# Two of the four weight sums of a seven-product tile, made by an adding transfer in a one-core encoder trunk

## The chip, the cores and the metric

The kernel runs on one core of a Trainium2 chip. The metric is the device time in microseconds (us) of one execution, as the median of several runs. The core has five engines that the text names as the profile does: PE (TensorE, matrix products; PEld is its loading of weights), DVE (VectorE), ACT (ScalarE), POOL (GpSimd) and SP (SyncE, which here only issues transfers). Each engine works through its own list of instructions in order, and waits on semaphores for others. Transfers between HBM and SBUF are issued by an engine's queue and carried out by 16 DMA engines.

## The reference

Two layers over 512 frames of 1024 channels: a pooling mixer and then a gated MLP with a causal convolution, chunked attention and then the same kind of MLP. The change lies in the MLP alone:

```python
def conv_ffn(h, w_gate, w_val, conv_w, conv_b, w_out):
    """out = (silu(causal_dwconv3(h W_gate)) * (h W_val)) W_out"""
    S = h.shape[1]
    a = h @ w_gate
    ap = jnp.pad(a, ((0, 0), (CONV_W - 1, 0), (0, 0)))
    a = ap[:, 0:S] * conv_w[0] + ap[:, 1:S + 1] * conv_w[1] + ap[:, 2:S + 2] * conv_w[2] + conv_b
    return (jax.nn.silu(a) * (h @ w_val)) @ w_out
```

The hidden width is 2816, which the kernel cuts into 22 channel tiles of 128.

## The kernel before

Channels lie on the 128 partitions, frames along the free axis. A float32 product is made as three passes over operands that are split into a high and a low part: `split` (L88) has ACT write the high part (L90) and DVE the low part (L91). So every weight chunk passes through ACT and DVE before PE can use it.

**Tiles of an FFN.** `KIND` says how a channel tile's gate and value are made. Tiles 0 to 4 are plain. Tiles 5 to 21, seventeen in each of the two FFNs, are made by `strassen` (L392): gate and value weights, each cut into the two halves of the inputs, form a 2 x 2 block matrix (a11, a12: gate; a21, a22: value), which meets 2 x 2 blocks of activations in seven products instead of eight. A product is 12 matmuls of 128 x 256, so a tile has 84 of them. Four sums of weights are needed, s1 = a21 + a22, s2 = s1 - a11, s3 = a11 - a21, s4 = a12 - s2; DVE makes them at L397 to L400 into two tiles, `sa` (s1, s2) and `sb` (s4, s3). The operands on the activations' side, t1 to t4, are made once for each FFN by `mixed` (L357), partly on POOL.

**Buffers.** The raw weights (gate, value, and the output projection's chunks `wo_r`) share three buffers (tag "wr"). `sa` and `sb` share two (tag "as"), so `sa` of a tile takes the buffer that `sa` of the tile before leaves when its parts are made. The parts come in pieces named by their place: g1 (the gate weights), g2 (`sa`), g3 (`sb`), g4 (a22); they go in turn into two buffer pairs of one ring and one of another.

**Order.** PE's order is written by hand: after each product of a tile some matmuls of the output projection of an earlier group of tiles are issued (`output`, L437), 128 x 512 each, summed into the residual X by DVE (L449). The other engines' orders are laid out beforehand by a scheduler from the data dependences. SP's queue issues all weight loads. A tile's results are x1 (product b11, copied from PSUM by ACT, L417), a (gate, L419 and L428), x5 (t1, L422), y (L424, L425) and v (value, L431 and L434); `hidden` (L300) then makes the convolution, the activation and the parts that the output projection takes.

Of the kernel before, what the change touches and what calls it, by code (L numbers as in the profile page):

```python
"""Hybrid trunk (pool mixer + FFN, chunked attention + FFN) on one NeuronCore.

Activations are kept feature-major: channels on partitions, the 512 frames along
the free axis, so that every projection takes its weights as the stationary operand,
the depthwise convolution and the pooling windows shift along the free axis, and no
transposes are needed between layers. A float32 product runs as three float32r passes
over operands that are split exactly into two 12-bit parts (hi + lo). Most of the FFN's gate
and value projections take seven products of half size instead of eight (Strassen).
"""
# [10 lines left out]
AF = mybir.ActivationFunctionType  # L20
# [23 lines left out]
# Attention: slots between the softmax of a query tile, its transpose and its use; slots by which the projections'  # L44
# products are done; the places of a pair's transposes among its slots.
# [4 lines left out]
# FFN: how a channel tile's gate and value are made (u: plain, from the inputs without 1/rms; p: plain; s: seven  # L50
# products), and the groups in which the hidden tiles enter the output projection.
# [15 lines left out]
def trunk(ctx: ExitStack, tc: tile.TileContext, xt, xT, cols, band, edge, poolw, gv, wout, wqk, wv, wo, rel, out):  # L67
# [9 lines left out]
    # Two banks of 16 float32r tiles that the stages use in turn.  # L77
# [3 lines left out]
    # ---------------------------------------------------------------- helpers  # L81
# [6 lines left out]
    def split(raw, hi, lo, eng=None):  # L88
        """raw = hi + lo, exactly."""
        nc.scalar.activation(hi, raw, AF.Copy)  # L90
        (eng or nc.vector).tensor_sub(lo, raw, hi.bitcast(F32))  # L91

    def split_scaled(src, scale, hi, lo):
        """The parts of src * scale (a column), from a tile in SBUF or PSUM."""
        nc.scalar.activation(hi, src, AF.Copy, scale=scale)
        nc.vector.scalar_tensor_tensor(lo, src, scale, hi.bitcast(F32), op0=OP.mult, op1=OP.subtract)

    def load_split(src, n, name, pool=None, eng=None, tag=(None, None)):
        """A weight chunk [P, n] and its two float32r parts."""
        raw = wp.tile([P, 1024], F32, name=f"{name}_r", tag="wr")  # L100
        if pool:
            hi, lo = (pool.tile([P, n], F32R, name=f"{name}_{c}", tag=t, bufs=2 if t == "as" else 1) for c, t in zip("hl", tag))
        else:
            hi, lo = (wp.tile([P, 1024], F32R, name=f"{name}_{c}", tag=f"w{c}", bufs=2) for c in "hl")
        nc.sync.dma_start(raw[:, :n] if len(src.shape) == 2 else raw.rearrange("p (a b) -> p a b", a=src.shape[1]), src)
        split(raw[:, :n], hi[:, :n], lo[:, :n], eng)
        return hi, lo

    def mm3(o, sh, sl, mh, ml, first, last):
        """o += (sh + sl).T @ (mh + ml), a matmul at a time"""  # L110
        yield nc.tensor.matmul(o, sh, mh, start=first, stop=False)  # L111
        yield nc.tensor.matmul(o, sh, ml, start=False, stop=False)  # L112
        yield nc.tensor.matmul(o, sl, mh, start=False, stop=last)  # L113
# [7 lines left out]
    def rsqrt(a, y, t):  # L121
        """y = a ** -0.5 on a small tile: a seed from exp(-log(a) / 2) and a Newton step."""
# [15 lines left out]
    def frame_rstd(acc, name):  # L138
        """1/rms of each frame, as columns [P, TT]."""
# [8 lines left out]
    def on_all(y, name):  # L148
        """The columns of y, [P, TT], as a row [P, S] on every partition."""
# [10 lines left out]
    # ---------------------------------------------------------------- pool mixer  # L160
    # The window means are products of the frame-major normed input with banded matrices.
    with tc.tile_pool(name="start", bufs=1) as sp:
# [14 lines left out]
        # The tensor engine's clock rises with use: these keep it busy until the input is there.  # L177
# [40 lines left out]
        # Frames [0, 256) come from frame tiles 0, 1; frames [256, 512) from 1, 2, 3.  # L218
# [25 lines left out]
        # Relative-position bias by distance, negated: row h holds, at u, distance u - 127, clipped.  # L244
# [10 lines left out]
    def prepare(XS, c, name):  # L255
        """The parts of x * g (1/rms is applied to the products), and 1/rms."""
        acc = g_tile(f"{name}_acc")
        for k in range(KD):
            split_scaled(X[k], col[:, c + k:c + k + 1], XS[k], XS[KD + k])
        for k in range(KD):  # L260
            sumsq(k, acc, name)
        return acc

    # ---------------------------------------------------------------- gated conv FFN
    # The gate and value projections multiply 2 x 2 blocks of weights (gate or value, halves of the inputs) by 2 x 2
    # blocks of activations (those halves, halves of the frames) in seven products (Strassen, in Winograd's form).
    def ffn(l, first, pool):
# [18 lines left out]
        def parts(raw, n, name, out_=False):  # L286
            """The parts of n columns of weights."""
# [12 lines left out]
        def hidden(f, a, finish):  # L300
            """The parts of silu(conv(a)) * val of a channel tile."""
# [12 lines left out]
        def early():  # L314
            """The first channel tiles, from the inputs without 1/rms."""
# [31 lines left out]
        def blocks(R):  # L347
            """The inputs times 1/rms, and their parts."""
            # They lie in tiles that the weights take later.
# [7 lines left out]
        def mixed(h, i):  # L357
            """The operands that mix blocks."""
# [3 lines left out]
            nc.gpsimd.tensor_sub(t1, b12, b11)  # L362
            nc.vector.tensor_sub(t2, b22, t1)
            nc.vector.tensor_sub(t3, b22, b12)
            nc.gpsimd.tensor_sub(t4, b21, t2)
# [3 lines left out]
        def whole(raw, i, j, names):  # L369
            """The parts of two moving operands, of the channel tiles i and i + 4."""  # L370
# [5 lines left out]
        def plain(f):  # L376
            """The gate and value of a channel tile; yields four times in each."""
# [14 lines left out]
        def strassen(f):  # L392
            """The gate and value of a channel tile; yields after each product."""
            g, v = (raw_tile(f"gv{l}_{f}_{i}", gv[l, f, i]) for i in range(2))
            sa, sb = (sum_tile(f"s{x}{f}") for x in "ab")
            a11, a12, a21, a22, s1, s2, s4, s3 = (x[:, z * S:(z + 1) * S] for x in (g, v, sa, sb) for z in range(2))
            nc.vector.tensor_add(s1, a21, a22)  # L397
            nc.vector.tensor_sub(s2, s1, a11)
            nc.vector.tensor_sub(s3, a11, a21)
            nc.vector.tensor_sub(s4, a12, s2)  # L400
# [20 lines left out]
            w = parts(sa, 1024, f"g2_{f}")  # L421
            nc.scalar.activation(x5, product(w, 0, "t1"), AF.Copy)  # L422
# [4 lines left out]
            w = parts(sb, 1024, f"g3_{f}")  # L427
            nc.vector.tensor_add(a[:, HALF:], y5, product(w, 0, "b22"))  # L428
            yield mm
            o = product(w, 1, "t3")[:, None, :].to_broadcast([P, 2, HALF])  # L430
            nc.vector.tensor_add(val.rearrange("p (h s) -> p h s", h=2), y.rearrange("p (h s) -> p h s", h=2), o)  # L431
# [6 lines left out]
        def output(g):  # L438
            """Adds a group's part of the output projection to the residual, a matmul at a time."""
# [41 lines left out]
    # ---------------------------------------------------------------- chunked attention  # L481
    def attention():
# [3 lines left out]
        # Softmax weights, transposed: [keys, (query tile of the half), key tile, query]; the key tile past  # L486
        # the first query tile's reach stays zero.
# [8 lines left out]
        def products(ov, w, name, eng=None):  # L496
            """ov[t] = the frames of tile t times the columns of w (two channel tiles to a chunk)."""
# [9 lines left out]
        def project(c, banks="PQ"):  # L507
            """Queries and keys of two head pairs, frame-major, with their norms (less the gains)."""
# [21 lines left out]
        def values(half, banks):  # L530
            ov = [psum(banks[t // 2], f"v{half}_{t}", BANKS[banks]) for t in range(TT)]
            yield from products(ov, wv[half], f"wv{half}")
            for t in range(TT):
                for hh in range(2):
                    V[t, 2 * half + hh] = vt = set1[(t * 2 + half) * 2 + hh].rearrange("p (h a d) -> p h a d", h=4, a=2)
                    v4 = ov[t][:, hh * 256:(hh + 1) * 256].rearrange("p (h d) -> p h d", d=HD)
                    # Even heads as [hi | lo], odd heads as [lo | hi].
# [3 lines left out]
        def output(ps_):  # L541
            """Adds the output projection of some of the head pairs to the residual."""
# [16 lines left out]
        def channel_major(p, i):  # L559
            """A pair's queries or keys, channel-major: by head, the queries' hi and lo parts and the keys' hi part twice,  # L560
            on the two halves of the partitions; the keys' lo parts."""
# [11 lines left out]
        def scores(h, t):  # L573
            """Softmax of the query tile t of a head."""
# [10 lines left out]
            # The scores and their bias come negated: their least is the softmax's maximum.  # L585
# [14 lines left out]
        def turn(h, t):  # L600
            """The softmax of a query tile, transposed, in parts."""
# [8 lines left out]
        def mix(h, m):  # L610
            """The values of half a head's frames, mixed."""
# [23 lines left out]
        # One query tile of a head to a slot; its stages lie slots apart, and the products of the next  # L635
        # projections stand between them.
# [4 lines left out]
        with tc.manual_schedule(engines={mybir.EngineType.PE}):  # L641
            cur, done, kept = 0, 0, 0

            def fill(upto):
                """Products of the projections, as many as are due by this point (in slots)."""
# [13 lines left out]
            for i in range(nb + LAG + LAGM):  # L659
# [14 lines left out]
                # The last projection leaves the parts of the input to those of the heads' outputs.  # L674
# [7 lines left out]
    # ---------------------------------------------------------------- program  # L682
# [60 lines left out]
```

## Time and profile before

| | |
|---|---|
| runs | 1034.02, 1032.58, 1029.66 us; median 1032.58 us |
| span of the profiled execution | 1030.7 us; no time of its own is given beside the span |
| DMA traffic | 105.31 MB, mean 102 GB/s |
| DVE sums of weights, L397 to L400 | 4 x 34 instructions of 128 x 512, about 684 ns each |

The span reaches from the first to the last instruction. Busy times of the engines overlap, so they don't add up to it; what an engine's work is worth depends on whether the engine that sets the end waits for it. "Idle before" in a row is the time in which its engine stood still just ahead of it, with the engine and line that ended the wait. A row of the timeline is start, duration, engine, line, operation, out<-in, shape. Instructions on an engine overlap a little, so the distance between two starts, not the duration, is what one costs a busy engine.

### The profile page before, as it was taken

Reading aid. Unit: us, or ns where it says so; the run is one execution under the profiler, and the core shown is the slowest. Engines: PE = TensorE matmul, PEld = TensorE weight load, DVE = VectorE, ACT = ScalarE, POOL = GpSimd, SP = SyncE. Lnnn points to the kernel's source line nnn. Section 1 sums busy time; section 2 is a strip of 40 time slices with the busy share of each in tenths; the row PEclk is TensorE's granted clock in tenths of the full one; section 3 lists DMA queues with packets and bytes.
Section 4 is the critical chain, followed back from the end, with each engine's and each line's share of the span. In section 5 each row is a group of like instructions: output and inputs, shape, how many; then the busy total and the mean of one; then the engine's idle time right before and its main releaser. Section 6 shows DMA issues by size and latency. Waiting matters only on the chain.

```text
span 1030.7 us, 15641 instructions
## 1 busy us (share of the span) xinstructions
PE 1011.2 (98%) x5928; PEld 871.2 (85%) x5928; DVE 815.3 (79%) x1407; ACT 536.3 (52%) x926; POOL 143.5 (14%) x140
## 2 busy tenths in 40 slices
PE   8899999999999999999899999999999999999998
PEld 7678999999999988887676767778899999999986
DVE  6889899988899754443767787889989998989843
ACT  5646554544445443345577867657554454444521
POOL 5413000000000013103324232052100000000000
PEclk8999999999999999999999999999999999999999
DMA  7213343333323234243233333222233333333323
GB/s 251 85 55 112 100 117 99 108 93 113 103 86 107 74 98 143 83 125 106 79 108 103 100 97 103 66 99 82 82 105 109 110 106 98 110 93 91 105 73 110
DMA packets 37724, 105.31 MB, mean 102 GB/s; under 512 B 4464, under 2 KB 6912, under 8 KB 37648
## 3 DMA queue, kind: packets, MB, share of 16 engines
q1 hardware_dynamic: 35984, 99.63, 32.3%
q0 software_dynamic: 1312, 4.24, 1.5%
q8 instruction: 47, 0.77, 0.3%
q10 hardware_dynamic: 352, 0.44, 0.1%
q14 instruction: 29, 0.24, 0.1%
HBM read 95.86 MB, written 2.14 MB: 95 GB/s over the span
## 4 chain that ended last, share of the span: by engine, by line
PE 89%; DVE 4%; issue 1%; ACT 1%; DMA 0%; DVEq 0%; ACTq 0%
PE out L111 8%; PE out L113 8%; PE out L112 8%; PE st_t L111 6%; PE st_t L112 6%; PE st_t L113 6%; PE st_b L111 5%; PE st_b L112 5%; PE st_b L113 5%; PE qk L111 3%; PE gv L112 3%; PE gv L113 3%; PE gv L111 3%; PE qk L113 3%; PE qk L112 3%; PE sc L588 2%
## 5 line engine op out<-in xcount | busy, mean ns | idle before, releaser
L90 ACT ACTIVATE g_h<-gv_r 128x1024 fp32r<-128x1024 f32 x68 | 57.6, 847 | 83.0 <-PE st_t L112 44.6
L113 PE MATMUL out<-one,ow_l 128*128 128x512 f32 x224 | 88.4, 394 | 0.0
L111 PE MATMUL out<-one,ow_h 128*128 128x512 f32 x224 | 88.3, 394 | 0.0
L112 PE MATMUL out<-one,ow_h 128*128 128x512 f32 x224 | 88.2, 394 | 0.0
L90 ACT ACTIVATE ow_h<-wo_r 128x640 fp32r<-128x640 f32 (+1 forms) x64 | 50.5, 788 | 65.4 <-PE out L112 48.5
L449 DVE TENSOR_TENSOR X<-out,X 128x512 f32<-128x512 f32 (+1 forms) x65 | 44.1, 680 | 42.0 <-PE out L113 41.8
L112 PE MATMUL st_t<-h,g_h 128*128 128x256 f32 x272 | 76.7, 282 | 0.0
L112 PE MATMUL st_t<-two,g_h 128*128 128x256 f32 x272 | 76.6, 282 | 0.0
L111 PE MATMUL st_t<-h,g_h 128*128 128x256 f32 x272 | 76.5, 281 | 0.0
L113 PE MATMUL st_t<-two,g_l 128*128 128x256 f32 x272 | 76.5, 281 | 0.0
L111 PE MATMUL st_t<-two,g_h 128*128 128x256 f32 x272 | 76.5, 281 | 0.0
L113 PE MATMUL st_t<-h,g_l 128*128 128x256 f32 x272 | 76.4, 281 | 0.0
L91 DVE TENSOR_TENSOR g_l<-gv_r,g_h 128x1024 fp32r<-128x1024 f32 x68 | 64.9, 954 | 4.9 <-ACT g_h L90 4.0
L90 ACT ACTIVATE g_h<-sa 128x1024 fp32r<-128x1024 f32 x34 | 36.1, 1060 | 59.0 <-PE st_t L112 45.3
L91 DVE TENSOR_TENSOR ow_l<-wo_r,ow_h 128x640 fp32r<-128x640 f32 (+1 forms) x64 | 56.6, 885 | 1.5 <-ACT ow_h L90 1.3
L112 PE MATMUL st_b<-h,g_h 128*128 128x256 f32 x204 | 57.5, 282 | 0.0
L112 PE MATMUL st_b<-two,g_h 128*128 128x256 f32 x204 | 57.4, 282 | 0.0
L111 PE MATMUL st_b<-two,g_h 128*128 128x256 f32 x204 | 57.4, 281 | 0.0
L111 PE MATMUL st_b<-h,g_h 128*128 128x256 f32 x204 | 57.4, 281 | 0.0
L113 PE MATMUL st_b<-two,g_l 128*128 128x256 f32 x204 | 57.4, 281 | 0.0
L113 PE MATMUL st_b<-h,g_l 128*128 128x256 f32 x204 | 57.2, 280 | 0.0
L306 DVE SCALAR_TENSOR_TENSOR c<-a,col,c 128x511 f32<-128x511 f32 x76 | 56.6, 745 | 0.1
(299 smaller groups left out, 3185.4 us busy)
## 6 DMA issues: line engine op xcount, KB each, us to landing
gv_r<-gv SPq DMA_DIRECT2D x88, 512.0 KB, 3.6
wo_r<-wout SPq DMA_DIRECT2D x32, 384.0 KB, 3.2
wo_r<-wout SPq DMA_DIRECT2D x32, 320.0 KB, 2.9
wqk_r<-wqk SPq DMA_DIRECT2D x16, 512.0 KB, 3.6
wv_r<-wv SPq DMA_DIRECT2D x8, 512.0 KB, 3.5
B<-rdram POOLq DMA_DIRECT2D x16, 256.0 KB, 3.6
wo_r<-wo SPq DMA_DIRECT2D x8, 512.0 KB, 3.7
z<-zh SPq DMA_DIRECT2D x24, 128.0 KB, 3.1
```

The source lines that it names most:

```text
L90: nc.scalar.activation(hi, raw, AF.Copy)
L91: (eng or nc.vector).tensor_sub(lo, raw, hi.bitcast(F32))
L111: yield nc.tensor.matmul(o, sh, mh, start=first, stop=False)
L112: yield nc.tensor.matmul(o, sh, ml, start=False, stop=False)
L113: yield nc.tensor.matmul(o, sl, mh, start=False, stop=last)
L306: nc.vector.scalar_tensor_tensor(c[:, j:], a[:, :S - j], cw[2 - j], c[:, j:], op0=OP.mult, op1=OP.add)
L449: nc.vector.tensor_add(X[d][:, fs], o[:, fs], X[d][:, fs])
L588: nc.tensor.matmul(sc[:, :nw], q[hs, t * P:n], kl[hs, :nw], start=False, stop=True)
```

## The change

`sa` now holds s3 and s1 and is filled by two transfers. The first, on SP's queue, writes a21 into both halves. The second, on POOL's queue, reads a11 and a22 from HBM and adds them to what lies there: s3 = a21 + a11, s1 = a21 + a22. It can be issued only when the first has landed. `sb` holds s4 and s2, still made by DVE: s2 = a11 + s1, s4 = a12 + s2. To make every weight sum an addition, the operands t1 to t4 change their signs, and so does the sign with which t3 enters the value. The product t3 now belongs to g2 and comes right after t1; before, it belonged to g3. The gate and value weights are loaded in full as before.

```diff
         def strassen(f):
             g, v = (raw_tile(f"gv{l}_{f}_{i}", gv[l, f, i]) for i in range(2))
             sa, sb = (sum_tile(f"s{x}{f}") for x in "ab")
-            a11, a12, a21, a22, s1, s2, s4, s3 = (x[:, z * S:(z + 1) * S] for x in (g, v, sa, sb) for z in range(2))
-            nc.vector.tensor_add(s1, a21, a22)
-            nc.vector.tensor_sub(s2, s1, a11)
-            nc.vector.tensor_sub(s3, a11, a21)
-            nc.vector.tensor_sub(s4, a12, s2)
+            a11, a12, a21, a22, s3, s1, s4, s2 = (x[:, z * S:(z + 1) * S] for x in (g, v, sa, sb) for z in range(2))
+            w0, w1 = gv[l, f, 0], gv[l, f, 1]
+            row, gap = w1.ap[0], w1.offset - w0.offset
+            sa3 = sa.rearrange("p (a b) -> p a b", a=2)
+            nc.sync.dma_start(sa3, bass.AP(tensor=w1.tensor, offset=w1.offset, ap=[row, [0, 2], [1, S]]))
+            nc.gpsimd.dma_start(sa3, bass.AP(tensor=w0.tensor, offset=w0.offset, ap=[row, [gap + S, 2], [1, S]]), accum_op=OP.add)
+            nc.vector.tensor_add(s2, a11, s1)
+            nc.vector.tensor_add(s4, a12, s2)
...
-            w = parts(sa, 1024, f"g2_{f}")
-            nc.scalar.activation(x5, product(w, 0, "t1"), AF.Copy)
+            ws = parts(sa, 1024, f"g2_{f}")
+            nc.scalar.activation(x5, product(ws, 1, "t1"), AF.Copy)
+            yield mm
+            w = parts(sb, 1024, f"g3_{f}")
+            o3 = product(ws, 0, "t3")[:, None, :].to_broadcast([P, 2, HALF])
             yield mm
             nc.vector.tensor_add(y6, x1, product(w, 1, "t2"))
             nc.vector.tensor_add(y5, y6, x5)
             yield mm
-            w = parts(sb, 1024, f"g3_{f}")
+            nc.vector.tensor_sub(val.rearrange("p (h s) -> p h s", h=2), o3, y.rearrange("p (h s) -> p h s", h=2))
             nc.vector.tensor_add(a[:, HALF:], y5, product(w, 0, "b22"))
-            yield mm
-            o = product(w, 1, "t3")[:, None, :].to_broadcast([P, 2, HALF])
-            nc.vector.tensor_add(val.rearrange("p (h s) -> p h s", h=2), y.rearrange("p (h s) -> p h s", h=2), o)
             w = parts(a22, 512, f"g4_{f}")
...
         def mixed(h, i):
...
-            nc.gpsimd.tensor_sub(t1, b12, b11)
-            nc.vector.tensor_sub(t2, b22, t1)
-            nc.vector.tensor_sub(t3, b22, b12)
-            nc.gpsimd.tensor_sub(t4, b21, t2)
+            nc.gpsimd.tensor_sub(t1, b11, b12)
+            nc.vector.scalar_tensor_tensor(t2, t1, -1.0, b22, op0=OP.mult, op1=OP.subtract)
+            nc.vector.tensor_sub(t3, b12, b22)
+            nc.gpsimd.tensor_add(t4, b21, t2)
```

In the changed program the transfers are L401 and L402, s2 is L403 and s4 L404; y is L431 and L432, v L434 and L438, a L423 and L435, X L453.

In DVE's list of before, between the low parts of g3 of tile 13 and those of g1 of tile 14 in the first FFN, the four sums of tile 14 stand spread among other work (u, c and X belong to `hidden` and `output`):

```order
L91 TENSOR_TENSOR g3_13_l_2415<-sb13_2318,g3_13_h_2414 128x1024
L306 SCALAR_TENSOR_TENSOR c12_2301<-a12_2145,col_124,c12_2301 128x510
L397 TENSOR_TENSOR sa14_2487<-gv0_14_1_r_2485 128x512
L399 TENSOR_TENSOR sb14_2488<-gv0_14_0_r_2483,gv0_14_1_r_2485 128x512
L398 TENSOR_TENSOR sa14_2487<-sa14_2487,gv0_14_0_r_2483 128x512
L435 TENSOR_TENSOR c12_2301<-v12_2148,c12_2301 128x512
L419 TENSOR_TENSOR a13_2323<-x13_2324,st0_13_b21_2348 128x256
L91 TENSOR_TENSOR g4_13_l_2451<-gv0_13_1_r_2315,g4_13_h_2450 128x512
L400 TENSOR_TENSOR sb14_2488<-gv0_14_0_r_2483,sa14_2487 128x512
L91 TENSOR_TENSOR u1l_509<-c12_2301,u1h_508 128x512
L449 TENSOR_TENSOR X2_74<-out0_1_2_2283,X2_74 128x512
```

In the changed DVE list the two sums that are left stand together, and from s2 to the low parts of g2 (made from `sa`) there are ten rows:

```order
L403 TENSOR_TENSOR sb14_2488<-gv0_14_0_r_2483,sa14_2487 128x512
L404 TENSOR_TENSOR sb14_2488<-gv0_14_0_r_2483,sb14_2488 128x512
L453 TENSOR_TENSOR X2_74<-out0_1_2_2283,X2_74 128x512
L91 TENSOR_TENSOR ow0_1_4_l_2537<-wo0_1_4_r_2534,ow0_1_4_h_2536 128x768
L91 TENSOR_TENSOR g1_14_l_2498<-gv0_14_0_r_2483,g1_14_h_2497 128x1024
L431 TENSOR_TENSOR y13_2325<-x13_2324,st0_13_t2_2416 128x256
L432 TENSOR_TENSOR y13_2325<-y13_2325,x13_2324 128x256
L434 TENSOR_TENSOR v13_2326<-st0_13_t3_2392,y13_2325 128x512
L435 TENSOR_TENSOR a13_2323<-y13_2325,st0_13_b22_2436 128x256
L91 TENSOR_TENSOR g2_14_l_2545<-sa14_2487,g2_14_h_2544 128x1024
```

The first sum moved from just behind c of tile 12 to behind the parts of `hidden` of tile 12 (u1l stands right ahead of it now), and it is the first DVE row that needs the transfers.

On SP's queue the new transfer of a tile stands between its weight loads, here for tiles 13 and 14 in the changed program:

```order
L277 DMA gv0_13_0_r_2313<-gv 128x1024
L401 DMA sa13_2317<-gv 128x2x512
L277 DMA gv0_13_1_r_2315<-gv 128x1024
L277 DMA wo0_1_3_r_2406<-wout 128x768
L277 DMA gv0_14_0_r_2483<-gv 128x1024
L277 DMA gv0_14_1_r_2485<-gv 128x1024
L401 DMA sa14_2487<-gv 128x2x512
L277 DMA wo0_1_4_r_2534<-wout 128x768
```

Of before, the same rows stood there without the two of L401; the queue waits at L401 until DVE has made the low parts of `sa` of the tile before, and the value load (tile 13) or the wout load (tile 14) stands behind it.

On POOL, the list of before goes from the operands t1 to t4 straight to the next stage; in the changed program the adding transfers follow, and the first one stands ahead of the last operands:

```order
L362 TENSOR_TENSOR t12_2_857<-hb_624 128x256
L365 TENSOR_TENSOR t34_2_858<-hh1_627,t12_2_857 128x256
L402 DMA sa5_971<-gv 128x2x512
L362 TENSOR_TENSOR t12_3_912<-hb_624 128x256
L365 TENSOR_TENSOR t34_3_913<-hl1_628,t12_3_912 128x256
L402 DMA sa6_1130<-gv 128x2x512
```

Behind these rows POOL's list holds nothing but the adding transfers of tiles 7 to 21 until the FFN ends.

## Prediction

> **What bounds the kernel now.** I read the page's busy times and chain first, then the waits of TensorE (PE), then the stretches by time.
>
> ```profile
> span 1030.7 us, 15641 instructions
> PE 1011.2 (98%) x5928; PEld 871.2 (85%) x5928; DVE 815.3 (79%) x1407; ACT 536.3 (52%) x926; POOL 143.5 (14%) x140
> PE 89%; DVE 4%; issue 1%; ACT 1%; DMA 0%; DVEq 0%; ACTq 0%
> ```
>
> PE is busy for 98% of the span and holds 89% of the chain that ended last. The waits of PE by releaser begin so, and all its rows together make about 15 us:
>
> ```profile
> PE tp L606 <- DVE mx L591: 4.9, 3, 2.4
> PE gv L112 <- DVE one L96: 4.1, 4, 2.3
> ```
>
> Neither is in a seven-product tile: L606 is attention, and the gv products of L112 that wait stand at the start of an FFN. Cut to 100 to 350 us, where the first FFN's seventeen such tiles run, the same view has no row at all. So VectorE (DVE) work that goes there has no PE wait to shorten. Could PE itself run quicker beside a less busy DVE? The stretches answer that (columns: PE, PEld, DVE, ACT, POOL busy with instruction counts, clock, DMA share, GB/s):
>
> ```profile
> 290.00:345.00 55.00, 55.00 (x394) 51.75 (x394) 50.88 (x78) 28.77 (x39) 0.00 (x0) 1.00 0.34 101
> 985.00:1025.00 40.00, 40.00 (x178) 32.48 (x177) 17.86 (x26) 8.77 (x12) 0.00 (x0) 1.00 0.32 98
> L111 PE MATMUL out<-one,ow_h 128*128 128x512 f32 x45 | 17.8, 395 | 0.0
> L113 PE MATMUL out<-one,ow_l 128*128 128x512 f32 x224 | 88.4, 394 | 0.0
> ```
>
> DVE is 93% busy in the first stretch and 45% in the second. The third row is an output matmul in the second stretch (395 ns), the fourth the like over the whole span (394 ns): a free DVE does not speed PE. The gain that this change can bring is therefore about nothing; the question is what the new transfers cost.
>
> **The change, part by part.** Removed are two DVE sums a tile:
>
> ```profile
> L397 DVE TENSOR_TENSOR sa<-gv_r 128x512 f32<-128x512 f32 x34 | 24.5, 721 | 12.0 <-DMA gv_r<-gv 11.8
> L399 DVE TENSOR_TENSOR sb<-gv_r,gv_r 128x512 f32<-128x512 f32 x34 | 23.2, 684 | 0.0
> ```
>
> That is 47.7 us of DVE time, all beside a PE that does not wait: worth 0 on the path. The matmuls stay 84 a tile; t3 before t2, the turned signs, and eight t2 operands as a scalar_tensor_tensor (128x256, some tenths of a us in all) lie beside PE work: 0.
>
> Added is a **loop from tile to tile**. sa of tile f+1 takes the buffer of sa of tile f, which is free when DVE has made the low parts of sa (g2 lo). Before, a plain sum filled it. Now, in turn: SP issues the first transfer; it lands; POOL issues the adding transfer; it lands; DVE runs s2 and, in order behind it, everything up to its next g2 lo. Only then can SP go on. While DVE waits at s2 (L403), g1 lo and the y, v, a sums are queued behind it, and PE waits for g1; ACT waits at the high parts of sa, with c, g3 and x copies behind; SP holds the val or wout load behind its sa transfer. Only the turns of this loop can cost time, when one is longer than PE's tile.
>
> PE's tile: x1 is copied once a tile. First and last of 17 copies in the first FFN:
>
> ```profile
> 104.91 0.39 ACT L417 ACTIVATE x<-st_b 128x256 f32<-128x256 f32 x1 [0.58 <-PE st_b L113]
> 342.06 0.39 ACT L417 ACTIVATE x<-st_b 128x256 f32<-128x256 f32 x1 [0.87 <-PE st_b L113]
> ```
>
> 237.15 us over 16 steps: **14.8 us a tile**.
>
> The DVE part of the loop, s2 to g2 lo, is priced by the distances between starts in a back-to-back piece of before:
>
> ```profile
> 261.04 0.69 DVE L91 TENSOR_TENSOR u3l<-c,u3h 128x512 fp32r<-128x512 f32 x1
> 261.64 0.41 DVE L424 TENSOR_TENSOR y<-x,st_t 128x256 f32<-128x256 f32 x1
> 261.97 0.68 DVE L449 TENSOR_TENSOR X<-out,X 128x512 f32<-128x512 f32 x1
> 262.57 1.22 DVE L91 TENSOR_TENSOR g_l<-gv_r,g_h 128x1024 fp32r<-128x1024 f32 x1
> 263.71 0.42 DVE L425 TENSOR_TENSOR y<-y,x 128x256 f32<-128x256 f32 x1
> 264.04 0.95 DVE L91 TENSOR_TENSOR ow_l<-wo_r,ow_h 128x768 fp32r<-128x768 f32 x1
> 264.91 0.41 DVE L428 TENSOR_TENSOR a<-y,st_b 128x256 f32<-128x256 f32 x1
> ```
>
> A 512 takes 0.60, a 256 0.33, a 768 0.87, a 1024 1.14. Tile 14's ten rows (above, under the change) make 4 x 0.60 + 3 x 0.33 + 0.87 + 1.14 + 1.22 for the last = 6.6 us. The same sum over the 16 loops of an FFN runs from 5.7 to 7.2; mean 6.2.
>
> The transfers:
>
> ```profile
> gv_r<-gv SPq DMA_DIRECT2D x88, 512.0 KB, 3.6
> wo_r<-wout SPq DMA_DIRECT2D x32, 320.0 KB, 2.9
> B<-rdram POOLq DMA_DIRECT2D x16, 256.0 KB, 3.6
> wo_r<-wo SPq DMA_DIRECT2D x8, 512.0 KB, 3.7
> L581 POOL DMA_DIRECT2D B<-rdram x16: 536/559/631, 399.8 to 637.6; - x16
> DMA to landing us min/median/max: 3.3/3.6/6.4
> ```
>
> A hand-over, read where SP takes up a freed buffer:
>
> ```profile
> 277.67 1.22 DVE L91 TENSOR_TENSOR g_l<-gv_r,g_h 128x1024 fp32r<-128x1024 f32 x1
> 278.92 1.74 SPq L277 DMA_DIRECT2D gv_r<-gv  x2
> ```
>
> DVE ends at 278.89 and SP issues 0.03 us later; I take 0.1 for each of four. The first transfer has the size and the 2 KB pieces of wo_r<-wo: 3.7 us. A turn is 3.7 + 0.4 + 6.2 + A = **10.3 + A**, and it hurts from A = 14.8 - 10.3 = **4.5 us** on.
>
> A, the adding transfer from issue to landing, is shown nowhere. The gv and wout rows give 0.7 us for 192 KB, so 1.9 us for 512 KB and 0.9 for 256. POOL's own transfer of 256 KB thus has 3.6 - 0.9 = 2.7 us besides data; a plain one of 512 KB would take 2.7 + 1.9 = 4.6. It also has twice the pieces (256 rows for 128), whose issue takes POOL 0.56 us for 128: up to 0.5 more. And an add must read the old SBUF contents, another 512 KB: between 0 (beside the first read) and 1.9 (after it). So A lies between 4.6 and 7.0; nearest is the middle, half of the second read: 2.7 + 1.9 + 0.5 + 0.9 = **6.0**. Outside bounds: below, 3.6, the half-size row itself; above, 8, its longest landing (6.4) plus 0.9 for the missing 256 KB and 0.7 for half a wout load in flight.
>
> The Trainium skill, "Collectives: The Full Stack", section "The bandwidth ceiling: the fold count and why AG ≠ RS ≠ AR", says that an adding transfer needs two source reads on the same ring and so runs at half the rate, 31 GB/s over two engines. That speaks against this change; an estimate from that page, 512 KB over 16 engines at that rate, is 2.1 us of data, A = 5.3 and some 20 us in all. No trace of before can show it.
>
> PE starts with a lead, read at the first tile:
>
> ```profile
> 102.56 1.22 DVE L91 TENSOR_TENSOR g_l<-sa,g_h 128x1024 fp32r<-128x1024 f32 x1
> 107.76 0.39 ACT L422 ACTIVATE x<-st_t 128x256 f32<-128x256 f32 x1 [0.34 <-PE st_t L113]
> ```
>
> g2 lo ends at 103.8. t1's twelve matmuls end just before 107.76 and, at 0.12 us each, began near 106.1: 2.3 us, and DVE has two sums (1.2 us) less there: 3.5, less 0.5 since g1 is a little tighter than g2: **3 us** for each FFN.
>
> Sum: 2 x (16 x (6.0 - 4.5) - 3) = 2 x 21 = **42 us**. 1030.7 + 42 = 1072.7 for the profiled execution; the median of the runs (1032.6) lies 1.9 above its span, so 1074.6, say **1075**.
>
> POOL's queue at the first tile: the adding transfer stands ahead of the last t1 operand.
>
> ```profile
> 86.10 0.41 DVE L364 TENSOR_TENSOR t<-hl,ha 128x256 f32<-128x256 f32 x1
> 91.64 1.12 POOL L362 TENSOR_TENSOR t<-hb 128x256 f32<-128x256 f32 x1 [2.96 <-DVE two L91]
> ```
>
> sa's buffer is free after L364, 86.5; plus 3.7 is 90.2, before 91.64: 0. Without that cover it would be a us or two, once in each FFN.
>
> **The rivals.**
>
> *Hidden (not slower).* If A is under 4.9, the turns fit: at 4.9 the sum is 2 x (6.4 - 3) = 7 us, about the 0.5% (5 us) that a measurement of this kernel can tell; at 4.5 it is 0, so 1032. For it: the plain estimate is 4.6, and the second read may run beside the first. Against: the pieces double, and the wout load is in flight then. The Trainium skill's "DMA: Bandwidth & Descriptors", section "Anatomy of one DMA — SWDGE (gpsimd) path", gives 2.0 us plus bytes at 436 GB/s, an estimate of 3.2 us here and no cost; by that rule the 256 KB row would be 2.6, and the trace has 3.6.
>
> *POOL starved.* POOL's work can be stretched beside DVE:
>
> ```profile
> 87.94 0.74 POOL L365 TENSOR_TENSOR t<-hh,t 128x256 f32<-128x256 f32 x1 [2.85 <-DVE t L363]
> 96.59 2.93 POOL L365 TENSOR_TENSOR t<-hl,t 128x256 f32<-128x256 f32 x1 [3.83 <-DVE t L363]
> ```
>
> The same instruction takes four times as long. If issuing were stretched so (1.1 to 4.4 us), A would be 9.3 and the sum 2 x (77 - 3) = 148: 1180. Against: POOL's issue in attention stayed within 536 to 631 ns.
>
> *Faster.* If the 47.7 us of DVE time let PE close gaps that the profile files elsewhere, at most about 5 us, 1027. PE's empty wait list for these tiles speaks against it.
>
> **How the numbers follow.** Forecast (A from 4.9 to 8): 0.62. Hidden: 0.27. Starved: 0.08. Faster: 0.03. At A = 8 the sum is 2 x (56 - 3) = 106: 1138. The range takes in hidden and forecast, 1031 to 1138; the forecast's own is 1040 to 1138. Faster by over 0.5%: 0.03; within: 0.27; slower: 0.70.
>
> **What would show it.** Right: x1 copies 16.3 us apart in place of 14.8; DVE's s2 (L403) idle before it, released by a DMA; PE rows at st_b waiting for g1's parts; sa from POOL landing in about 6 us. Wrong: no PE wait in these tiles (A under 4.5); or period and A long, but DVE not waiting at L403, which would put the loop elsewhere, such as in SP's queue.

## The result and the profile after

The changed kernel takes **1138.3 us** (median of 4 runs, 1135.98 to 1142.52) against 1031.9 (4 runs of the kernel before beside it): a ratio of 1.105, 95% interval 1.101 to 1.109. The forecast was 1075, slower; the direction and the mechanism came true, the size did not, and the time lies 0.3 us above the range's upper end of 1138. The span of the profiled execution is 1140.7, 110.0 more than before.

The page of the profile after, cut to what answers the rows of before:

```profile
span 1140.7 us, 15771 instructions
PE 1048.0 (92%) x5928; PEld 899.2 (79%) x5928; DVE 776.6 (68%) x1339; ACT 528.1 (46%) x926; POOL 181.7 (16%) x174
...
q0 software_dynamic: 10560, 22.06, 11.1%
...
PE 42%; DVE 24%; DMA 20%; issue 6%; ACT 2%; DVEq 0%; POOLq 0%; ACTq 0%
...
L403 DVE TENSOR_TENSOR sb<-gv_r,sa 128x512 f32<-128x512 f32 x34 | 23.5, 692 | 189.5 <-DMA sa<-gv 179.1
L113 PE MATMUL st_b<-two,g_l 128*128 128x256 f32 x204 | 66.2, 324 | 73.2 <-DVE g_l L91 73.2
...
sa<-gv SPq DMA_DIRECT2D x34, 512.0 KB, 3.8
sa<-gv POOLq DMA_DIRECT2D x34, 512.0 KB, 7.3
wo_r<-wout SPq DMA_DIRECT2D x32, 384.0 KB, 4.0
```

PE's 89% of the chain has become 42%, and DVE and DMA hold 44%. The row of L403 is the reason: s2 stands idle for 179.1 us until the transfers have filled sa. PE then waits 73.2 us for the low parts of g1, which stand behind s2 in DVE's queue; before, PE had no wait in these tiles. The other 37 us of the 110 show in PE's row as busy time (1048.0 against 1011.2), at a mean granted clock of 0.964 against 0.993; more on it at the end. DVE did lose its two sums (776.6 us busy against 815.3) and nobody gained by it.

One turn of the loop, from the timelines of SP, POOL and DVE in the profile after (the rows between are left out):

```profile
269.37 0.38 SPq L401 DMA_DIRECT2D sa<-gv  x1
...
273.48 1.20 POOL L402 DMA_DIRECT2D sa<-gv  x1 [17.38 <-DMA sa<-gv]
...
281.19 0.69 DVE L403 TENSOR_TENSOR sb<-gv_r,sa 128x512 f32<-128x512 f32 x1 [5.45 <-DMA sa<-gv]
...
286.10 1.22 DVE L91 TENSOR_TENSOR g_l<-sa,g_h 128x1024 fp32r<-128x1024 f32 x1
...
287.35 0.38 SPq L401 DMA_DIRECT2D sa<-gv  x1
```

First transfer to POOL's issue 4.1 us, adding transfer to s2 7.7, s2 to the end of g2 lo 6.1, and SP issues the next 0.03 later: 18.0 us. The x1 copies of the first FFN show the same step:

```profile
104.75 0.39 ACT L421 ACTIVATE x<-st_b 128x256 f32<-128x256 f32 x1
...
396.85 0.36 ACT L421 ACTIVATE x<-st_b 128x256 f32<-128x256 f32 x1
```

292.1 us over 16 steps are 18.3 us a tile; it was 14.8, and 16.3 was forecast. The mean of all 32 turns, from the same rows of every tile, is 18.5. In none of the 32 does DVE stand idle for 0.1 us or more between s2 and the end of g2 lo, and SP's issue follows 0.02 to 0.03 us behind. So the turn closes through transfers, POOL and DVE alone: PE does not lengthen it, however slow its matmuls are.

### The profile page after: what moved, and what is told of

Same layout as the page of the kernel before. It is cut to its first block, busy times and chain, and to the rows that moved or that the text cites. A ratio compares the mean times of both kernels' runs of the same rounds, so it can differ in the third digit from the quotient of the medians.

```text
span 1140.7 us, 15771 instructions
## 1 busy us (share of the span) xinstructions
PE 1048.0 (92%) x5928; PEld 899.2 (79%) x5928; DVE 776.6 (68%) x1339; ACT 528.1 (46%) x926; POOL 181.7 (16%) x174
## 3 DMA queue, kind: packets, MB, share of 16 engines
q0 software_dynamic: 10560, 22.06, 11.1%
## 4 chain that ended last, share of the span: by engine, by line
PE 42%; DVE 24%; DMA 20%; issue 6%; ACT 2%; DVEq 0%; POOLq 0%; ACTq 0%
DMA sa<-gv 18%; DVE g_l L91 7%; PE out L112 3%; PE out L113 3%; PE out L111 3%; PE qk L111 3%; DVE c L306 3%; PE qk L113 2%; PE qk L112 2%; DVE ow_l L91 2%; PE gv L112 2%; DVE sb L403 2%; PE gv L111 2%; PE gv L113 2%; PE sc L592 2%
## 5 line engine op out<-in xcount | busy, mean ns | idle before, releaser
L403 DVE TENSOR_TENSOR sb<-gv_r,sa 128x512 f32<-128x512 f32 x34 | 23.5, 692 | 189.5 <-DMA sa<-gv 179.1
L113 PE MATMUL st_b<-two,g_l 128*128 128x256 f32 x204 | 66.2, 324 | 73.2 <-DVE g_l L91 73.2
L402 POOL DMA_DIRECT2D sa<-gv x34 | 40.9, 1204 | 541.7 <-DVE a L423 142.3
L113 PEld LDWEIGHTS st_b<-two,g_l 128*128 128x128 f32 x204 | 43.4, 213 | 79.2 <-DVE g_l L91 79.1
L304 ACT ACTIVATE c<-a,col 128x512 f32<-128x512 f32 x38 | 31.0, 816 | 139.8 <-DVE a L435 133.5
L113 PE MATMUL out<-one,ow_l 128*128 128x512 f32 x224 | 91.1, 407 | 0.0
L112 PE MATMUL out<-one,ow_h 128*128 128x512 f32 x224 | 90.9, 406 | 0.0
L111 PE MATMUL out<-one,ow_h 128*128 128x512 f32 x224 | 90.4, 403 | 0.0
L453 DVE TENSOR_TENSOR X<-out,X 128x512 f32<-128x512 f32 (+1 forms) x65 | 44.0, 678 | 38.8 <-PE out L113 38.8
L112 PE MATMUL st_b<-h,g_h 128*128 128x256 f32 x204 | 62.2, 305 | 0.0
L111 PE MATMUL st_b<-h,g_h 128*128 128x256 f32 x204 | 62.2, 305 | 0.0
L113 PE MATMUL st_b<-h,g_l 128*128 128x256 f32 x204 | 62.0, 304 | 0.0
L111 PE MATMUL st_b<-two,g_h 128*128 128x256 f32 x204 | 61.3, 300 | 0.0
```

The lines of the kernel that those rows point to most:

```text
L304: nc.scalar.activation(c, a, AF.Identity, scale=cw[2], bias=cw[3])
L402: nc.gpsimd.dma_start(sa3, bass.AP(tensor=w0.tensor, offset=w0.offset, ap=[row, [gap + S, 2], [1, S]]), accum_op=OP.add)
L403: nc.vector.tensor_add(s2, a11, s1)
L453: nc.vector.tensor_add(X[d][:, fs], o[:, fs], X[d][:, fs])
```

## The experiments

The theory is that the serial loop (sa free, first transfer, adding transfer, s2 to g2 lo) sets the tile and so the time. The rivals: the new order and signs; the added load on the DMA engines or a slower PE; and, for the size, what makes the adding transfer take 7.3 us and not 6.0. Intervals are 95% intervals of the ratio to the kernel before, run beside them. The times of the kernel before in these comparisons were 1032.4 (the first four experiments below), 1032.0 (the one with no load in the tiles) and 1031.5 (the other four).

### The order and signs alone

```diff
-            nc.sync.dma_start(sa3, bass.AP(tensor=w1.tensor, offset=w1.offset, ap=[row, [0, 2], [1, S]]))
-            nc.gpsimd.dma_start(sa3, bass.AP(tensor=w0.tensor, offset=w0.offset, ap=[row, [gap + S, 2], [1, S]]), accum_op=OP.add)
+            nc.vector.tensor_add(s1, a21, a22)
             nc.vector.tensor_add(s2, a11, s1)
+            nc.vector.tensor_add(s3, a11, a21)
             nc.vector.tensor_add(s4, a12, s2)
```

> Signs, operands and product order of the change, but all four sums by VectorE again, no added transfers. Loop theory (the serial loop sa free, first transfer, adding transfer, VectorE's stretch to g2 lo sets the tile): no loop, a tile of 14.8 us as before, 1032 (1028 to 1037). Rival 'order' (the new product order or signs cost part of the 106 us): above 1037, up to 1138 if they are all of it.

1032.4 us, ratio 0.9998 (0.998 to 1.002). Order and signs cost nothing; all of the 106 us comes from the transfers.

### s2 and s4 behind g2 lo

Here low[0] is the instruction that made the last low parts.

```diff
-            nc.vector.tensor_add(s2, a11, s1)
-            nc.vector.tensor_add(s4, a12, s2)
...
             ws = parts(sa, 1024, f"g2_{f}")
+            with tc.issue_after(low[0].ins):
+                nc.vector.tensor_add(s2, a11, s1)
+                nc.vector.tensor_add(s4, a12, s2)
```

> All transfers of the change with the same buffers, but s2 and s4 stand behind g2 lo in VectorE's queue, so that VectorE's stretch in the loop shrinks from 6.6 us to about 2.5 (high parts 1.2, low parts 1.2). Loop theory: turn 4.6 + 7.3 + 2.5 = 14.4 against PE's 14.8, so 1032 to 1050, depending on queueing on ScalarE. Rival 'load' (35 MB more traffic or POOL's issuing slows PE's loads or its clock): 1138 as in the change. Rival 'transfer term only' (the stretch on VectorE doesn't count): 1138 too.

1059.8 us, ratio 1.027 (1.023 to 1.031): three quarters of the loss is gone with every transfer and buffer in place, only by the order of DVE's queue. So neither the load nor the transfers by themselves make the 106 us. The time is 10 us above the expected band. The timelines of one turn show two things that were overlooked. DVE's, at g2 lo:

```profile
272.82 1.22 DVE L91 TENSOR_TENSOR g_l<-sa,g_h 128x1024 fp32r<-128x1024 f32 x1
273.96 0.69 DVE L426 TENSOR_TENSOR sb<-gv_r,sa 128x512 f32<-128x512 f32 x1
```

SP's, from there on:

```profile
274.71 0.38 SPq L402 DMA_DIRECT2D sa<-gv  x1
276.27 0.33 SPq L278 DMA_DIRECT2D gv_r<-gv  x1
280.22 0.33 SPq L278 DMA_DIRECT2D wo_r<-wout  x1
```

And ScalarE's, at the high parts of sa:

```profile
286.29 0.84 ACT L90 ACTIVATE ow_h<-wo_r 128x768 fp32r<-128x768 f32 x1 [5.15 <-DMA wo_r<-wout]
287.04 1.05 ACT L90 ACTIVATE g_h<-sa 128x1024 fp32r<-128x1024 f32 x1
```

s2 reads sa as well, and now comes last, so sa is free 0.7 us later than g2 lo (273.96 + 0.69 = 274.65, and SP goes on at 274.71). And ScalarE takes the wout parts ahead of the high parts of sa: the wout load, issued at 280.22, was there at 286.29, after 6.1 us, nearly all of them beside the adding transfer (issued at 278.99, landed 7.1 us later). The turns have a mean of 16.1 us.

### A third buffer for the sums

`into` is a sum buffer of its own, allotted ahead of ha and hb.

```diff
-            return pool.tile([P, 1024], F32R, name=name, tag="as", bufs=2).bitcast(F32)
+            return pool.tile([P, 1024], F32R, name=name, tag="as", bufs=3).bitcast(F32)
...
-        R = big.tile([P, S], F32, name=f"{name}_R")
+        R = into[:, :S]
```

> All transfers of the change and its order, but three buffers in place of two for the sums (1/rms on all partitions moves into one of them, before its use as a sum), so that sa of the next tile waits for a sum of the tile before last. Loop theory: one turn now spans two tiles, 4.6 + 7.3 + about 9 = 21 us against 29.6, so hidden: 1028 to 1037, granted clock back near 0.99. Rival 'load': 1100 to 1138, clock 0.96.

1033.6 us, ratio 1.002 (0.9996 to 1.004), granted clock 0.993. Who waits for POOL's transfer in this kernel, and its landing time (shortest, median, longest), from the view of line 402:

```profile
who waited for it (us, times):
  DVE sb L403: 1.8, 2
DMA to landing us min/median/max: 5.7/6.1/9.6
```

And PE's row, from its waits:

```profile
PE st_b L113 <- DVE g_l L91: 1.3, 3, 0.8
```

The same 68 transfers and the same bytes are all there, and the adding ones take 5.7 to 9.6 us each, but almost nobody waits: 1.8 us in place of 179.1. It is the reuse of sa's buffer that turns the transfers into time, not their load. And with them hidden, DVE's saved sums gain nothing either, as step one of the prediction had it.

### The same transfers without the add

```diff
-            nc.gpsimd.dma_start(sa3, bass.AP(tensor=w0.tensor, offset=w0.offset, ap=[row, [gap + S, 2], [1, S]]), accum_op=OP.add)
+            nc.gpsimd.dma_start(sa3, bass.AP(tensor=w0.tensor, offset=w0.offset, ap=[row, [gap + S, 2], [1, S]]))
```

> POOL's transfer overwrites in place of adding (the sums s1 and s3 are left out), bytes, pieces, queues and waits unchanged. Issue to landing, A, was 7.3 us with the add. My reading (issuing 1.2 of 256 pieces, data 1.9, fixed 2.7) gives A = 5.5 to 6 without it, a turn of 16.7 to 17.2 and 2 x (16 x 1.9 to 2.4 - 3) = 55 to 71: 1087 to 1103. If the add costs nothing: A stays 7.3 and the time 1138. If the add is nearly all of what exceeds the 3.6 us of the 256 KB row: A = 4.6, turn 15.8, 1059.

1062.4 us, ratio 1.030 (1.025 to 1.035), below the value expected and near the 1059 of its last case: the add costs more than I took. From its page:

```profile
q0 software_dynamic: 6208, 22.06, 6.8%
...
L402 POOL DMA_DIRECT2D sa<-gv x34 | 24.6, 725 | 487.8 <-DVE c L439 157.3
...
sa<-gv POOLq DMA_DIRECT2D x34, 512.0 KB, 4.7
```

And the view of line 402:

```profile
DMA to landing us min/median/max: 3.9/4.7/6.7
```

Against the change (10560 packets of q0, 1.20 us of issuing, 7.3 us), this one has 4352 packets less, 128 for each of 34 transfers. So it wasn't only the add that went: without the 1312 packets that q0 has before the change, a plain transfer has 144 and an adding one 272, and POOL issues the plain one in 0.73 us. Its shortest landing is 3.9 us, that of the adding one 5.8: together the add and its packets cost 1.9 us between the two shortest, 0.5 of it in issuing. The mean turn is 16.2 us.

### Half the size

```diff
-            nc.sync.dma_start(sa3, bass.AP(tensor=w1.tensor, offset=w1.offset, ap=[row, [0, 2], [1, S]]))
-            nc.gpsimd.dma_start(sa3, bass.AP(tensor=w0.tensor, offset=w0.offset, ap=[row, [gap + S, 2], [1, S]]), accum_op=OP.add)
+            nc.sync.dma_start(s1, bass.AP(tensor=w1.tensor, offset=w1.offset, ap=[row, [1, S]]))
+            nc.gpsimd.dma_start(s1, bass.AP(tensor=w1.tensor, offset=w1.offset + S, ap=[row, [1, S]]), accum_op=OP.add)
             nc.vector.tensor_add(s2, a11, s1)
             nc.vector.tensor_add(s4, a12, s2)
+            nc.vector.tensor_add(s3, a11, a21)
```

> Only s1 is made by transfers (256 KB, one piece a row, first and adding transfer both half as large); s3 by VectorE, ahead of s2 in its queue. Loop theory: first transfer and hand-over 2.9 + 0.6, adding transfer about 4.5 (7.3 less half of issuing, 0.6, and half of both reads, 1.9, and of what the loads add), VectorE 6.6: turn 14.6 against 14.8, so 1028 to 1045. Rival 'fixed cost' (an adding transfer costs about 7 us at any size): turn 17, 1090.

1056.6 us, ratio 1.026 (1.021 to 1.030): too slow for the loop theory's band and far too fast for a fixed cost. The transfers came out as expected:

```profile
sa<-gv SPq DMA_DIRECT2D x34, 256.0 KB, 2.9
sa<-gv POOLq DMA_DIRECT2D x34, 256.0 KB, 4.1
```

What was wrong is DVE's stretch, 7.9 us from s2 to g2 lo in place of 6.6. An example from its timeline:

```profile
288.25 0.96 DVE L91 TENSOR_TENSOR ow_l<-wo_r,ow_h 128x768 fp32r<-128x768 f32 x1 [1.70 <-ACT ow_h L90]
```

With s2 earlier, the work queued behind it meets its own waits inside the stretch, here for the parts of a wout load. But over the 32 turns such waits make a mean of only 0.28 us. The larger part of the 1.3 us is more work: the stretch holds a mean of 11.3 instructions in place of 9.5, above all work of `hidden` (its low parts and c), which the change does ahead of s2 in most turns, and s3 in 8 of the 32. The loop shrank by 2.7 us, not by 3.9.

### What the adding transfer meets

In the change, POOL's transfers take 5.8 to 9.1 us. Two of them follow, each from the view of line 402 with the rows of SP's timeline from 2 us before to 4 us after it. The first:

```profile
L402 POOL DMA_DIRECT2D sa<-gv x1: 1194/1194/1194, 144.2 to 144.2; - x1
...
DMA to landing us min/median/max: 5.9/5.9/5.9
```

SP beside it:

```profile
143.62 0.33 SPq L277 DMA_DIRECT2D wo_r<-wout  x1
```

The second:

```profile
L402 POOL DMA_DIRECT2D sa<-gv x1: 1194/1194/1194, 847.4 to 847.4; - x1
...
DMA to landing us min/median/max: 9.1/9.1/9.1
```

SP beside it:

```profile
847.35 0.33 SPq L277 DMA_DIRECT2D gv_r<-gv  x1
848.89 0.33 SPq L277 DMA_DIRECT2D wo_r<-wout  x1
```

Over the 34, those with one load issued from 2 us before to 4 us after POOL's issue (26) have a mean of 6.8 us, those with two (8) 8.5. That suggests that the price over 6.0 is the loads beside it.

Where do these loads come from? DVE and SP behind the g2 lo of the turn shown above, in the change:

```profile
272.65 0.95 DVE L91 TENSOR_TENSOR ow_l<-wo_r,ow_h 128x768 fp32r<-128x768 f32 x1
273.62 0.33 SPq L277 DMA_DIRECT2D gv_r<-gv  x1
274.44 0.69 DVE L91 TENSOR_TENSOR g_l<-gv_r,g_h 128x512 fp32r<-128x512 f32 x1
275.16 0.33 SPq L277 DMA_DIRECT2D wo_r<-wout  x1
```

Each load comes 0.02 to 0.03 us after DVE has made low parts and so freed a raw buffer. All 42 loads issued within these 6 us around POOL's issue come within 0.08 us behind such a row (32 of them behind the low parts of g4), 3.5 to 6.1 us after SP has issued the first transfer. So it isn't SP's place at L401 that holds them back, but DVE's work right behind g2 lo, which lasts about as long as the first transfer.

Three kernels try what the loads cost. The first loads wout once per FFN:

```diff
+                if not once:
+                    once.append(pool.tile([P, GM * P], F32, name=f"wo{l}"))
+                    nc.sync.dma_start(once[0], wout[l, 0, :, :GM * P])
-                w = parts(raw_tile(f"wo{l}_{g}_{d}", wout[l, d, :, b * P:(b + m) * P], n), n, f"ow{l}_{g}_{d}", True)
+                w = parts(once[0], n, f"ow{l}_{g}_{d}", True)
```

> The change with one wout load per FFN in place of 32: all output products of an FFN take that load's weights (the others are left out); the splits and products stay. Theory 'collisions' (5.9 us is the adding transfer alone, the rest of its mean of 7.3 are the loads that the loop releases beside it): adding transfer down to 6 to 6.5, first transfer to 3.7, turn 17.0 to 17.5, 1090 to 1105. Rival 'own cost' (7.3 is the transfer's own): turn stays 18.4, 1130 to 1140.

The second issues each wout load twice, the second time right behind the first (last[0]):

```diff
+                more = pool.tile([P, GM * P], F32, name=f"wm{l}_{g}_{d}", tag="wm", bufs=1)
+                with tc.issue_after(last[0].ins):
+                    nc.sync.dma_start(more[:, :n], src)
```

> The change with each wout load issued twice, the second into a buffer that nobody reads (12 MB more in all). Theory 'collisions': adding transfer up by 0.7 to 1.5 us, turn 19.2 to 20, 1160 to 1190. Rival 'own cost': no change, 1138.

The third leaves out the gate and value loads of the seven-product tiles too:

```diff
-            g, v = (raw_tile(f"gv{l}_{f}_{i}", gv[l, f, i]) for i in range(2))
+            if len(once) < 3:
+                once[1:] = [raw_tile(f"gv{l}_{f}_{i}", gv[l, f, i]) for i in range(2)]
+            g, v = once[1:]
```

> As the kernel with one wout load per FFN, and the seventeen seven-product tiles of an FFN also share one gate and one value load (the other weights are left out): both transfers for the sums stay, with no load beside them. Theory 'collisions': adding transfer 5.9 us, first transfer 3.6 and hand-over 0.6, VectorE 6.2 to 6.6, turn 16.3 to 16.7, by 2 x (16 x (turn - 14.8) - 3) 1073 to 1086. Rival 'own cost' (6.9 us, as it was with the gate and value loads beside it, is the transfer's own): turn 17.4, 1104.

Times: 1104.1 us (ratio 1.070, 1.067 to 1.074) with one wout load, 1166.0 (1.132, 1.127 to 1.137) with twice as many, 1068.3 (1.036, 1.031 to 1.041) with no load in the tiles. The landing of the adding transfer, from the view of its line, with one wout load:

```profile
DMA to landing us min/median/max: 5.8/7.2/8.5
```

With twice as many:

```profile
DMA to landing us min/median/max: 5.9/8.0/10.1
```

And with none:

```profile
DMA to landing us min/median/max: 5.7/5.9/7.7
```

The first is a half miss: its time lies where expected, but the transfer fell only to a mean of 6.9 us, not to 6 to 6.5, since now each of them meets a gate or value load; the rest came from the first transfer (4.3 to POOL's issue, was 4.6) and from DVE (6.2, was 6.6). Taken alone it would have left the question open. The third decides it: with no load beside it the transfer takes a median of 5.9 us, in the same loop, and 8.0 with the doubled loads (64 loads and 23 MB more; the 12 MB expected was too low). Two of its 33 transfers without a load still took 7.5 and 7.7 us, for a reason that stays open.

The count over 6 us hides that it matters when a load comes. With the third buffer, all but one of the 34 adding transfers have a load in these 6 us, 26 of them two or three, and yet their median is 6.1 us. In a narrower stretch, set after the fact from 0.7 us before to 1.3 us after POOL's issue, 11 of them have one load (mean 8.1 us) and 23 none (6.0). In the change it is 27 with one (7.2) and 4 with none (5.9). The difference is smaller in the kernel with s2 behind g2 lo (7.5 against 6.7), so the edges of the stretch aren't sharp.

### The first transfer replaced by a copy

```diff
-            nc.sync.dma_start(sa3, bass.AP(tensor=w1.tensor, offset=w1.offset, ap=[row, [0, 2], [1, S]]))
+            nc.scalar.activation(sa3, a21[:, None, :].to_broadcast([P, 2, S]), AF.Copy)
```

> The first transfer is replaced by a copy of a21 into both halves by ScalarE (about 1.1 us, and 1 to 2 us of queue ahead of it); adding transfer, buffers and VectorE's order as in the change. Loop theory: the term of 4.6 us becomes 2.6 to 3.6, turn 16.5 to 17.5, 1075 to 1107. Rival 'adding transfer alone' (the first transfer is hidden): 1138.

1083.7 us, ratio 1.052 (1.048 to 1.057). The time is in the band, for other reasons than expected. From g2 lo to POOL's issue it took a mean of 5.3 us, more than the 4.6 of the transfer, as the copy waits 3.9 us for its place in ScalarE's queue. The turn fell to 16.8 because the adding transfer meets fewer loads near its issue (median 6.0 us; 24 of 34 have none from 0.7 us before to 1.3 after) and because DVE's stretch is shorter (5.2), as work that stood behind s2 is now done ahead of it. That the first transfer lies on the path is thus not shown by this run; that it does is read from the timelines alone.

### The terms side by side

Means of 32 turns, in us, from the rows of each tile in the timelines: end of g2 lo to POOL's issue; that to s2; s2 to the end of g2 lo; the turn; the median time. The kernel with s2 behind g2 lo has another loop and the one with a third buffer has none of this kind, so they aren't in the table.

| kernel | to POOL's issue | adding transfer to s2 | s2 to g2 lo | turn | time |
|---|---|---|---|---|---|
| forecast | 3.9 | 6.1 | 6.3 | 16.3 | 1075 |
| the change | 4.6 | 7.3 | 6.6 | 18.5 | 1138.3 |
| wout loads twice | 4.8 | 8.0 | 6.6 | 19.4 | 1166.0 |
| one wout load | 4.3 | 6.9 | 6.2 | 17.4 | 1104.1 |
| no loads | 4.3 | 6.0 | 6.2 | 16.5 | 1068.3 |
| copy by ScalarE | 5.3 | 6.3 | 5.2 | 16.8 | 1083.7 |
| no add | 4.7 | 4.9 | 6.6 | 16.2 | 1062.4 |
| half the size | 3.5 | 4.4 | 7.9 | 15.8 | 1056.6 |

The time goes with the turn and with no single term: 2 x 16 x (turn - 14.8), less 8 to 20 us for both FFNs together, gives how far each profiled span lies over that of before (1030.7).

## Why the prediction missed

**The gain of nothing** was right: 47.7 us less of DVE's work bring nothing where the transfers are hidden (ratio 1.002).

**The order and signs at nothing** were right (0.9998).

**The loop** was right in its links and in what it does: x1 copies farther apart, s2 idle before a DMA, PE waiting at st_b for g1's parts; and a third buffer removes all of it. The threshold of 14.8 us was not tested: no kernel with this loop has a mean turn under 15.8. The spans fit it, with 8 to 20 us off for both FFNs where 6 were forecast.

**The size** is where it failed: the turn was 18.5, not 16.3, and a tenth of a us in the turn costs 3.2 us. Three terms were too small. (1) A was taken as 6.0, and measured a mean of 7.2; with its hand-over 7.3 against my 6.1: +1.2, or 39 us. For the transfer alone the value was near, 5.9 with no loads, but partly by luck: the plain part was reckoned at 4.6 and takes 3.9 at the shortest, the add and its pieces at 1.4 and they cost 1.9. Missing was the load beside it. I had written that SP holds the val or wout load behind its sa transfer, and yet counted such a load only in the outer bound of 8, as if it were a mishap. It is the rule, and not by SP's queue: the loads wait for raw buffers, which DVE frees right behind g2 lo, so they come out just as POOL's transfer starts. (2) First transfer and hand-overs: 4.6 against 3.9, +0.7, or 23 us. The transfer landed after a mean of 4.0 us, not 3.7; it took 3.7 in the two kernels without the wout loads. And POOL issued 0.57 us after the landing where I took 0.1, a value read from a hand-over from DVE to SP. (3) DVE's stretch with its hand-over: 6.6 against 6.3, +0.3, or 9 us. The distances that I added up come from neighbours that don't need each other's results. In the change three pairs do, and their starts lie farther apart: s2 to s4 0.73 us where they are neighbours (26 turns) in place of 0.60, the first y to the second 0.45 and the second y to v 0.46, both in place of 0.33. That is about all of the difference. These 71 us on top of 42 make 113, less the lead, which came out 1 or 2 us longer for each FFN than the 3 forecast: the 110 of the span.

**The range** ended at 1138 because its upper end moved A alone, to 8, and left the other terms at their middle. A of 7.2 with the other two terms as measured gives about the same time.

**The rivals.** "Hidden" fell: A never went below 5.7 us for the 512 KB. By the constants of the Trainium skill's "DMA: Bandwidth & Descriptors", section "Anatomy of one DMA — SWDGE (gpsimd) path", an estimate is 3.2 us; the adding transfer has 5.9 alone, and even the plain one 3.9. "Starved" fell: POOL's issuing took 1.19 to 1.26 us in the change, twice that of 128 pieces and not four times. The Trainium skill's "Collectives: The Full Stack", section "The bandwidth ceiling: the fold count and why AG ≠ RS ≠ AR", says of the adding step of a collective that it is slower for its second read. The 1.9 us between the plain and the adding transfer don't contradict that, but no run here shows a second read: 0.5 of them is issuing, and the packets changed too. The estimate made from its figures, 5.3 us, is 0.6 under the 5.9.

## What to carry to other kernels

When work is moved from an engine to a chain of transfers, follow the buffer: if the next tile's transfers wait for the last read of this tile's, latency that a queue would hide becomes the period of the loop, and one buffer more is worth more than a faster transfer (here 1.002 of the time before against 1.026 for half the size and 1.030 without the add); the reader's place in its queue was worth about as much (1.027). Price a transfer in such a loop beside the loads that come out at the same point of the turn, not by its landing time alone; and when a range is made, move all terms that share a cause together. Before any of this, ask whether the relieved engine was waited for: here it wasn't.

## What the hardware showed beside this

An adding transfer can be cut into pieces that a plain one isn't: 128 packets more for each transfer of 512 KB with the same addresses, two pieces a row, with 1.20 us of issuing in place of 0.73. At 256 KB, one piece a row, the adding transfer has the 144 packets that the plain one has at 512 KB, and issuing takes 0.87. The hand-over from a landed DMA to POOL's next issue was 0.57 us, that from ScalarE to POOL 0.30, and from DVE to SP 0.03.

The granted clock was lower where PE's share was: 0.974 at 94% busy (one wout load), 0.964 at 92% (the change) and 0.956 at 91% (wout twice), while at 95% to 98% it stayed at 0.989 to 0.997. The trace of the change shows where it falls. PE's first matmul behind its wait in the turn above, and four stretches around it (the clock stands third from the right):

```profile
266.42 0.58 PE L113 MATMUL st_b<-two,g_l 128*128 128x256 f32 x1 [4.94 <-DVE g_l L91]
258.00:262.00 4.00, 3.48 (x23) 2.96 (x21) 0.00 (x0) 1.79 (x2) 0.00 (x0) 1.00 0.61 110
266.00:270.00 4.00, 3.58 (x14) 3.30 (x14) 3.93 (x8) 1.76 (x3) 0.00 (x0) 0.50 0.72 229
270.00:274.00 4.00, 4.00 (x24) 3.77 (x23) 4.00 (x7) 2.23 (x5) 0.52 (x1) 0.76 0.43 131
274.00:278.00 4.00, 4.00 (x29) 3.70 (x28) 1.74 (x4) 1.93 (x3) 0.68 (x1) 1.00 0.81 168
```

Behind the wait of 4.94 us the clock is half for about 5.5 us: the matmuls of 128 x 256 start 0.21 us apart, and 0.12 later on. The same stands behind 11 of the 30 waits of more than 0.3 us that PE has in these tiles, for 3 to 6 us each, after waits of 1.8 to 4.9 us; behind others, up to 3.9 us long, it does not, so no threshold follows. The lower clock comes after the waits, and PE is no part of the turn: here it is an effect of the loop, not a part of the cause.
